# A two-layer encoder kernel: the order of five instruction streams worked out back from the products

## The chip, the cores and the metric

One NeuronCore of a Trainium2 chip runs the whole kernel in one launch. The core has four compute engines, each with its own instruction stream: TensorE (PE in the profile, with its weight loads as PEld) for products and transposes, VectorE (DVE), ScalarE (ACT) and GpSimd (POOL) for work on elements; a fifth stream, SyncE (SP), issues the transfers. Products are written to PSUM, which is used here as eight banks of 128 x 512 floats; everything else lives in SBUF. The metric is the device time of one execution in microseconds, as the median of the runs.

## The reference

Two encoder layers over 512 tokens of width 1024, then a last RMS norm. All inputs are float32. Each layer does, cut to what matters:

```python
h = rms_norm(x, norm_mix)
na_q, na_k, na_v, g_q, g_k, g_v = split(h @ w_in)           # 8 heads each, 64 wide; g_k, g_v have 2
na  = softmax(na_q @ na_k.T / 8 + bias, masked to a window of 8 rows x 16 columns) @ na_v
g_q, g_k = rope(rms_norm(g_q)), rope(rms_norm(g_k))         # per head
gqa = softmax(g_q @ g_k.T / 8) @ g_v                        # 4 query heads share one key head
x = x + concat(na, gqa) @ w_out
x = x + softmax(q @ k.T / sqrt(128)) @ v @ w_mem_o          # q from rms_norm(x), k and v from 256 memory tokens
u = conv3(rms_norm(x) @ w_up)                               # width 3 over the positions, 5632 columns
x = x + (silu(u[:2816]) * u[2816:]) @ w_down
```

## The kernel before

**Products.** A float32 product is made of three faster ones: every operand is split into a rounded part `hi` (type fp32r) and the rest `lo`, and PE adds hi x hi, hi x lo and lo x hi into one PSUM bank. A weight tile arrives in `raw` by a transfer that SP issues; ACT casts it to `hi` (L269, in one or two halves), and POOL, sometimes DVE, subtracts to make `lo` (L270). Both have four buffers, `raw` has two. The activations are held transposed, as operands `xg` (L439, L442). Before a cast can write `hi`, the products that read this buffer's last tile have to be done; before a product can start a new group, its PSUM bank has to be free. There are four banks for products and transposes of attention (`mm`), two for scores (`sc`), two for transposes and small sums (`tr`).

**Stages.** In each layer the neighbourhood heads and the grouped-query heads come first (about 40 to 343 us of the span in the first layer, 686 to 1017 in the second, with the memory attention at their end), then the FFN (343 to 686 and 1017 to 1330). The projections of one head group are woven with the attention of another: a `Filler` hands out products of a projection in portions while softmax work of the former heads goes on.

**The steps that the following parts name.** In the neighbourhood attention L762 adds the bias and reduces, L768 takes the exponential on ACT, L774 and L780 normalise, and the values' products are evicted by a copy on ACT (L814) and two operations on DVE (L815, L816), of which the last one frees the `mm` bank. A grouped-query projection is evicted by L866 and L867 on DVE and L868 on ACT, normalised by L878, L884, L885, L889, rotated and added up by L899, and split by L703 and L705. Grouped-query scores are reduced by L924 (DVE), put through the exponential by L926 (ACT), inverted by L932 (DVE), scaled by L491 (POOL) and, transposed by PE, copied to operands by L484 (ACT) and L485 (DVE). L849 evicts the values, L537 scales a memory operand.

**What sets the order.** PE's products and SP's transfers stand in the order in which the program emits them: their engines are wrapped, and every instruction is pinned.

```python
    def __getattr__(self, name):                      # class InOrder
        op = getattr(self.engine, name)
        return lambda *a, **k: self.tc.keep_in_program_order(op(*a, **k))
```

DVE, POOL and most of ACT are ordered by the framework's scheduler, which plays the program through with its own costs and takes the ready instruction of the best priority. Two devices lean on it: `behind(n)` sets a weight cast back by n places in priority, and `issue_after(closed[-1])` keeps the casts of three kinds of weights (memory queries, FFN up, keys) behind the last closed group.

## Time and profile before

| | |
|---|---|
| time, median of 3 runs (lowest, highest) | 1372.61 us (1371.69, 1373.6) |
| span of the profiled execution, the time it stands for | 1373.2 us |
| instructions | 19238 |
| busy: PE, PEld, DVE, ACT, POOL | 1350.8, 1154.6, 873.9, 676.8, 689.6 us |
| granted TensorE clock, mean | 0.997 |
| transfers | 139.88 MB, mean 102 GB/s |

The page gives no time of the profiled execution but its span, which lies 0.6 us above the median of the runs and among them. A busy share says how long an engine had anything to do; where PE is the engine that is always busy, its idle time between products, with what it waits for, is what is left over.

### The profile page before, as it was taken

What the parts mean: (1) busy time and instruction counts of PE and PEld (TensorE: products, weight loads), DVE (VectorE), ACT (ScalarE), POOL (GpSimd) and SP (SyncE); (2) the same over time, 40 slices, a digit from 0 to 9 for tenths busy, and PEclk for the clock granted to TensorE, in tenths of its full rate; (3) what the DMA queues carried; (4) which work ended last, traced back from release to release, by engine and by line L of the source; (5) the groups of instructions that cost most, each with busy time, mean ns of one, the idle gap of its engine ahead of it and who ended that gap; (6) DMA issues with size and microseconds to landing.
All of it is one profiled execution on the core that took longest, in us unless ns stands there. A gap on an engine that the chain in (4) does not pass through costs nothing.

```text
span 1373.2 us, 19238 instructions
## 1 busy us (share of the span) xinstructions
PE 1350.8 (98%) x7068; PEld 1154.6 (84%) x7068; DVE 873.9 (64%) x1540; ACT 676.8 (49%) x1258; POOL 689.6 (50%) x493
## 2 busy tenths in 40 slices
PE   9999999999999999999999999999999999999997
PEld 7998799888888888888888978998788888888897
DVE  6676675565886188268546767745758833861874
ACT  6775676564543243233457657755554422432441
POOL 2566656626444443444544666657264444444441
PEclk9999999999999999999999999999999999999999
DMA  6763213222333332332265531133143333333331
GB/s 214 230 167 95 62 47 93 84 70 78 107 93 95 104 93 85 107 99 84 86 183 179 150 88 54 57 99 92 32 123 92 93 108 92 93 92 108 92 93 62
DMA packets 219358, 139.88 MB, mean 102 GB/s; under 512 B 6144, under 2 KB 212224, under 8 KB 219264
## 3 DMA queue, kind: packets, MB, share of 16 engines
q1 hardware_dynamic: 218160, 137.99, 34.2%
q8 instruction: 56, 0.92, 0.3%
q10 hardware_dynamic: 1104, 0.66, 0.2%
q14 instruction: 38, 0.31, 0.1%
HBM read 126.05 MB, written 2.10 MB: 93 GB/s over the span
## 4 chain that ended last, share of the span: by engine, by line
PE 90%; DVE 4%; ACT 2%; POOL 1%; DMA 1%; issue 1%; ACTq 0%; DVEq 0%; POOLq 0%
PE mm L76 80%; PE sc L76 6%; PE tr L63 3%; PE tr L76 1%; POOL lo L270 1%; DVE mm L428 1%; DVE xT L429 1%; DMA raw<-in_w_in 0%; ACT hi L269 0%; ACT t L768 0%; DVE r L705 0%; DVE s L924 0%; DVE xg L485 0%; DMA raw<-in_w_mem_q 0%; DVE t L815 0%
## 5 line engine op out<-in xcount | busy, mean ns | idle before, releaser
L270 POOL TENSOR_TENSOR lo<-raw,hi 128x1024 fp32r<-128x1024 f32 (+2 forms) x268 | 500.2, 1877 | 478.0 <-ACT hi L269 477.8
L76 PE MATMUL mm<-xg,hi 128*128 128x512 f32 x1920 | 595.6, 391 | 3.6 <-DVE t L816 2.1
L76 PEld LDWEIGHTS mm<-xg,hi 128*128 128x128 f32 x1920 | 356.3, 188 | 74.7 <-issue 2.3
L269 ACT CAST hi<-raw 128x512 fp32r<-128x512 f32 (+2 forms) x276 | 224.0, 835 | 329.4 <-PE mm L76 271.5
L76 PE MATMUL mm<-xg,lo 128*128 128x512 f32 x960 | 374.0, 390 | 0.0
L76 PE MATMUL mm<-r,hi 128*128 128x512 f32 (+1 forms) x1144 | 331.6, 374 | 2.0 <-DVE xg L442 1.6
L76 PEld LDWEIGHTS mm<-r,hi 128*128 128x128 f32 x1144 | 207.1, 189 | 40.3 <-DVE xg L442 3.3
L1238 DVE SCALAR_TENSOR_TENSOR t<-t,par,t 128x7 f32<-128x7 f32 (+1 forms) x352 | 201.9, 641 | 34.0 <-ACT t L1231 34.0
L76 PE MATMUL mm<-r,lo 128*128 128x512 f32 (+1 forms) x572 | 212.9, 372 | 0.0
L76 PEld LDWEIGHTS mm<-xg,lo 128*128 128x128 f32 x960 | 180.5, 188 | 38.2
L76 PEld LDWEIGHTS mm<-r,lo 128*128 128x128 f32 x572 | 107.8, 188 | 18.8
L1223 DVE TENSOR_TENSOR t<-mm,rep 128x512 f32<-128x512 f32 x88 | 60.1, 687 | 77.7 <-PE mm L76 62.1
L491 POOL TENSOR_SCALAR t<-t,s 128x512 f32<-128x512 f32 (+1 forms) x112 | 66.7, 610 | 72.9 <-DVE s L932 39.6
L1244 DVE TENSOR_TENSOR r<-t,r 128x512 fp32r<-128x512 f32 x44 | 90.4, 2056 | 7.4 <-ACT r L1243 4.3
L1240 ACT ACTIVATE t<-t 128x512 f32<-128x512 f32 x44 | 27.9, 633 | 134.7 <-DVE t L1238 134.6
L1267 DVE TENSOR_TENSOR xT<-xT,mm 128x512 f32<-128x512 f32 x32 | 21.9, 685 | 106.8 <-PE mm L76 106.8
L76 PE MATMUL sc<-r,r 128*128 128x256 f32 (+1 forms) x352 | 71.0, 334 | 1.7 <-ACT t L926 1.7
L1231 ACT ACTIVATE t<-t,par 128x512 f32<-128x512 f32 x88 | 66.8, 806 | 3.3 <-DVE t L1223 3.3
L63 PE MATMUL tr<-ident,t 128*128 128x128 f32 x456 | 63.1, 276 | 3.3 <-DVE s L932 1.2
L63 PEld LDWEIGHTS tr<-ident,t 128*128 128x128 f32 x456 | 53.1, 142 | 12.7 <-issue 5.8
L76 PE MATMUL mm<-r,r 128*128 128x256 f32 (+1 forms) x428 | 62.0, 297 | 0.6 <-DVE r L705 0.6
L76 PEld LDWEIGHTS mm<-r,r 128*128 128x128 f32 x428 | 56.2, 191 | 3.2 <-DVE r L705 0.8
(153 smaller groups left out, 1571.7 us busy)
## 6 DMA issues: line engine op xcount, KB each, us to landing
raw<-in_w_up SPq DMA_DIRECT2D x88, 512.0 KB, 3.7
raw<-in_w_in SPq DMA_DIRECT2D x33, 512.0 KB, 4.2
raw<-in_w_down SPq DMA_DIRECT2D x32, 448.0 KB, 3.6
raw<-in_w_mem_kv SPq DMA_DIRECT2D x16, 512.0 KB, 3.8
raw<-in_w_down SPq DMA_DIRECT2D x16, 512.0 KB, 3.9
r<-in_bias SPq DMA_DIRECT2D x16, 384.0 KB, 5.6
r<-r SPq DMA_DIRECT2D x22, 256.0 KB, 5.1
raw<-in_w_out SPq DMA_DIRECT2D x8, 512.0 KB, 3.6
```

Of the source, the lines that this page charges most:

```text
L63: return lambda *a, **k: self.tc.keep_in_program_order(op(*a, **k))
L76: return self.tc.keep_in_program_order(self.engine.matmul(out, lhsT, rhs, **k))
L269: act.copy(hi[:, k], raw[:, k])
L270: (POOL if eng[0] == "P" else DVE).tensor_sub(lo[:, k], raw[:, k], f(hi)[:, k])
L428: DVE.tensor_add(pm, pm, xT[c])
L491: eng.tensor_scalar(e, e, sums[:, col : col + 1], 1.0, op0=ALU.mult, op1=ALU.mult)
L1223: DVE.tensor_mul(u, us[side], ffn.rep)
L1231: ACT.activation(cc, u, AF.Identity, bias=par[:, l, CB + ch : CB + ch + 1], scale=w[1])
L1238: DVE.scalar_tensor_tensor(cc[:, dst], u[:, src], wi, cc[:, dst], op0=ALU.mult, op1=ALU.add)
L1240: ACT.activation(cs[0], cs[0], AF.Silu)
L1244: DVE.tensor_sub(acts[j][1], cs[0], f(acts[j][0]))
L1267: DVE.tensor_add(xT[m], xT[m], pm)
```

## The change

After the whole program has been emitted, and ahead of the framework's own pass, `put_in_order` makes an order for all five streams. It reads every instruction with the tiles that it reads and writes, and gives each a busy time and a latency from a table of costs by engine, kind and width. From start times of the products (at first PE without any idle time) `due` works back through everything that feeds a product, and through the buffers and banks that have to be free, to the latest time at which each instruction may start. `run` then plays the program forward: an engine takes, among the instructions that could start within its `patience`, the one that is due first; PE takes the first in the program's order among those that could start within 60 ns, and looks 300 instructions ahead. This is done for six plans (with SP's order given or free, and with margins of 0, 40 or 80 ns) and twice for each, from the former round's starts. Each order is then played three times with every operation up to 4% longer and up to 80 ns late at random, and the one of the lowest mean is kept. It is forced on the framework as a chain of dependencies without synchronisation, one per engine. The pins of `InOrder` and the gate `issue_after` go; `behind` stays. The two names `InOrder` and `Counted` remain as plain wrappers. No instruction is added or taken away, but a cast that stood as two halves one after the other can now have other work between.

```diff
 class InOrder:
     def __getattr__(self, name):
         op = getattr(self.engine, name)
-        return lambda *a, **k: self.tc.keep_in_program_order(op(*a, **k))
+        return op
...
+PLANS = [
+    ((60.0, 300.0, 300.0, 300.0, 0.0), 300, given, margin) for given in ((), (E_SP,)) for margin in (0.0, 40.0, 80.0)
+]
...
+    def due(self, start):
+        later = [[] for _ in self.steps]
+        for tag, tiles in self.opened.items():
+            for a, b in zip(tiles, tiles[self.bufs[tag]:]):
+                first = self.users[b][0]
+                for x in self.users[a]:
+                    if x < first:
+                        later[x].append(first)
...
+        for s in reversed(self.steps):
+            long = HANDOVER + (s.busy + LANDING + s.moved / BYTES_PER_NS if s.moved else s.length)
+            for x in s.frees:
+                same = self.steps[x].engine == s.engine and not s.moved
+                at[s.i] = min(at[s.i], at[x] - (s.busy if same else long))
+            for x in later[s.i]:
+                at[s.i] = min(at[s.i], at[x] - long)
+        return at
...
+                if e in held:
+                    i = program[e][head[e]]
+                    among = (i,) if not todo[i] else ()
+                else:
+                    reach = program[e][min(head[e] + ahead, len(program[e]) - 1)] if e == E_PE else len(steps)
+                    among = [i for i in open_to[e] if i <= reach]
...
+                if can:
+                    soon = min(can)[0] + patience[e]
+                    _, t, i = min((due[i] if due and e != E_PE else i, t, i) for t, i in can if t <= soon)
...
+def put_in_order(tc):
...
+    for patience, ahead, given, margin in PLANS:
+        at = start
+        for _ in range(2):
+            r = course.run(course.due(at), patience, ahead, given, margin)
...
+            under = [course.run(None, (0.0,) * 5, 0, order=r[2], rng=np.random.default_rng(n)) for n in range(3)]
...
+            mean = sum(u[0] for u in under) / len(under)
+            if best is None or mean < best[0]:
+                best = mean, r[2]
+    order = best[1]
+    follows = mybir.DependencyInfo(mybir.DependencyClass.NoSync, mybir.DependencyReason.DATA)
+    for engine in order:
+        for a, b in zip(engine, engine[1:]):
+            tc.add_manual_dep(course.steps[b].ins, course.steps[a].ins.name, follows, reason="put_in_order")
...
-                with tc.issue_after(closed[-1]) if closed and key[0] in ("memq", "up", "k") else nullcontext():
-                    act.copy(hi[:, k], raw[:, k])
+                act.copy(hi[:, k], raw[:, k])
...
     with tile.TileContext(nc, schedule_with_timeline_sim=True) as tc:
         encoder_kernel(tc, t, out)
+        put_in_order(tc)
```

What it makes of the order at three places; a row reads line, operation, output <- inputs with the numbers of the tiles, and shape. The lines of the changed kernel have other numbers, since the planner stands ahead of them.

**Third query projection of the second layer, about 804 us of the span, DVE.** `mm_7572` and `mm_7580` are the two banks with the products of the attention values, `t_7570` their result; `mm_7603` holds the rotated queries, `t_7601` the grouped-query values. Before:

```order
L878 SCALAR_TENSOR_TENSOR s_7564<-tr_7559,geps 128x8
L899 TENSOR_TENSOR mm_7603<-t_7441,mm_7603 128x512
L815 TENSOR_TENSOR t_7571<-mm_7572,t_7571 64x2x128
L815 TENSOR_TENSOR t_7571<-mm_7580,t_7571 64x2x128
L816 TENSOR_TENSOR t_7570<-mm_7572,t_7571 64x256
L849 TENSOR_TENSOR t_7601<-mm_7522,rep_6368 128x512
L816 TENSOR_TENSOR t_7570<-mm_7580,t_7571 64x256
```

Now (L1096 and L1097 are L815 and L816, L1130 is L849, L1180 is L899, L766 is L485):

```order
L1096 TENSOR_TENSOR t_7571<-mm_7572,t_7571 64x2x128
L1097 TENSOR_TENSOR t_7570<-mm_7572,t_7571 64x256
L1130 TENSOR_TENSOR t_7601<-mm_7522,rep_6368 128x512
L1180 TENSOR_TENSOR mm_7603<-t_7441,mm_7603 128x512
L766 TENSOR_TENSOR r_7634<-tr_7629,r_7634 128x512
L1096 TENSOR_TENSOR t_7571<-mm_7580,t_7571 64x2x128
L1097 TENSOR_TENSOR t_7570<-mm_7580,t_7571 64x256
```

The eviction of the first bank moved ahead of L899, and that of the second bank behind it. On ACT the copies L814 of both banks moved ahead of the cast of `hi_7694`.

**The same place, PE.** `mm_7616` is the projection that takes over a bank of the values, `tr_7629` and `tr_7637` are transposes. Before:

```order
L76 MATMUL mm_7616<-xg_5998,hi_7420 128x512
L76 MATMUL mm_7616<-xg_5999,hi_7420 128x512
L76 MATMUL mm_7616<-xg_5998,lo_7421 128x512
L63 MATMUL tr_7629<-ident,t_7409 128x128 x4
L63 MATMUL tr_7637<-ident,t_7410 128x128 x4
```

Now:

```order
L77 MATMUL mm_7603<-ident,t_7454 128x128 x4
L1071 MATMUL tr_7629<-ident,t_7409 128x128 x4
L1071 MATMUL tr_7637<-ident,t_7410 128x128 x3
L77 MATMUL mm_7616<-xg_5998,hi_7420 128x512
L77 MATMUL mm_7616<-xg_5999,hi_7420 128x512
L77 MATMUL mm_7616<-xg_5998,lo_7421 128x512
```

Six products of the projection stood ahead of the eight transposes; now seven of the eight stand ahead of the projection.

**First layer, about 120 us, ACT.** `sc_1381` and `sc_1382` are scores of the neighbourhood attention, `mm_1320` is the projection that L868 evicts, `hi_1525` and `hi_1437` are weight casts. Before:

```order
L269 CAST hi_1525<-raw_1318 128x512 x2
L768 ACTIVATE t_1393,s_1392<-sc_1381,s_1391 128x256 x2
L768 ACTIVATE t_1394,s_1392<-sc_1382,s_1391 128x256 x2
L868 ACTIVATE t_1410<-mm_1320 128x512
L814 COPY t_1415<-mm_1416 64x2x128
L814 COPY t_1415<-mm_1424 64x2x128
```

Now (L1049 is L768, L550 is L269, L1149 is L868, L1095 is L814):

```order
L550 CAST hi_1437<-raw_1214 128x512 x2
L1049 ACTIVATE t_1393,s_1392<-sc_1381,s_1391 128x256
L1049 ACTIVATE t_1394,s_1392<-sc_1382,s_1391 128x256
L1049 ACTIVATE t_1393,s_1392<-sc_1381,s_1391 128x256
L1049 ACTIVATE t_1394,s_1392<-sc_1382,s_1391 128x256
L550 CAST hi_1525<-raw_1318 128x512
L1149 ACTIVATE t_1410<-mm_1320 128x512
L1095 COPY t_1415<-mm_1416 64x2x128
L1095 COPY t_1415<-mm_1424 64x2x128
```

The four exponentials moved ahead of the cast of `hi_1525`, and its second half behind the evictions. On PE the scores moved 42 rows ahead.

**First layer, about 154 us, ACT.** `sc_1767` and `sc_1768` are grouped-query scores, `sc_1806` and `sc_1807` the next ones, which take over their banks. `hi_1998` takes over the buffer of `hi_1525`, which the products of `mm_1781` read. Before:

```order
L926 ACTIVATE t_1776,s_1774<-sc_1767,s_1773 128x512
L926 ACTIVATE t_1779,s_1774<-sc_1768,s_1773 128x512
L926 ACTIVATE t_1815,s_1813<-sc_1806,s_1812 128x512
L926 ACTIVATE t_1818,s_1813<-sc_1807,s_1812 128x512
L269 CAST hi_1998<-raw_1732 128x512 x2
```

Now (L1207 is L926, L984 is L703):

```order
L550 CAST hi_1998<-raw_1732 128x512
L1207 ACTIVATE t_1776,s_1774<-sc_1767,s_1773 128x512
L1207 ACTIVATE t_1779,s_1774<-sc_1768,s_1773 128x512
L550 CAST hi_1998<-raw_1732 128x512
L984 CAST r_1887<-mm_1827 64x512
L1207 ACTIVATE t_1815,s_1813<-sc_1806,s_1812 128x512
L1207 ACTIVATE t_1818,s_1813<-sc_1807,s_1812 128x512
```

One half of the cast moved ahead of the exponentials of the first pair, the other ahead of the second pair. On PE the order at this place is, before:

```order
L63 MATMUL tr_1789<-ident,t_1717 128x128 x4
L63 MATMUL tr_1796<-ident,t_1720 128x128 x4
L76 MATMUL sc_1806<-r_1506,r_1635 128x512 x2
L76 MATMUL sc_1807<-r_1507,r_1635 128x512 x2
L76 MATMUL mm_1781<-r_1502,hi_1525 128x512 x2
L76 MATMUL mm_1781<-r_1502,lo_1526 128x512
L76 MATMUL mm_1781<-r_1722,hi_1525 128x512 x2
L76 MATMUL mm_1781<-r_1722,lo_1526 128x512
```

Now (`mm_1841` is the projection group that follows `mm_1781`, `mm_1827` another transpose):

```order
L1228 MATMUL tr_1789<-ident,t_1717 128x128 x4
L77 MATMUL mm_1781<-r_1722,hi_1525 128x512
L1228 MATMUL tr_1796<-ident,t_1720 128x128 x4
L77 MATMUL mm_1781<-r_1722,hi_1525 128x512
L77 MATMUL mm_1781<-r_1722,lo_1526 128x512
L77 MATMUL mm_1827<-ident,t_1681 128x128 x4
L77 MATMUL mm_1841<-r_934,hi_1611 128x512 x2
L77 MATMUL mm_1841<-r_934,lo_1612 128x512
L77 MATMUL sc_1806<-r_1506,r_1635 128x512 x2
```

The rest of `mm_1781` and the first products of `mm_1841` moved ahead of the scores `sc_1806`.

## The prediction

> **What bounds the kernel now.** I read the busy times and the chain that ended last first, then the windows by stage, then TensorE's (PE's) waits, and then the timeline at the longest of them.

> ```profile
> PE 1350.8 (98%) x7068; PEld 1154.6 (84%) x7068; DVE 873.9 (64%) x1540; ACT 676.8 (49%) x1258; POOL 689.6 (50%) x493
> PE 90%; DVE 4%; ACT 2%; POOL 1%; DMA 1%; issue 1%; ACTq 0%; DVEq 0%; POOLq 0%
> ```

> PE is busy for 98% of the span and holds 90% of the chain; no other engine is above 64%. So an order can bring only what PE loses between products, and that is found stage by stage. In the windows the columns are the stretch, its length, the busy time of PE, PE's weight loads, VectorE (DVE), ScalarE (ACT) and GpSimd (POOL), then the granted clock, the DMA share and GB/s.

> ```profile
> 0.00:40.00 40.00, 37.23 (x181) 31.50 (x182) 27.23 (x48) 26.45 (x47) 12.30 (x15) 1.00 0.63 196
> 40.00:343.00 303.00, 296.12 (x1757) 258.29 (x1757) 195.26 (x417) 189.15 (x426) 181.51 (x166) 1.00 0.35 103
> 343.00:686.00 343.00, 343.00 (x1515) 284.12 (x1515) 217.50 (x301) 131.91 (x172) 155.15 (x71) 1.00 0.33 96
> 686.00:1017.00 331.00, 326.32 (x1918) 285.54 (x1918) 207.91 (x435) 202.06 (x445) 191.41 (x174) 0.99 0.36 105
> 1017.00:1330.00 313.00, 313.00 (x1416) 260.62 (x1415) 202.94 (x280) 117.96 (x150) 138.40 (x59) 1.00 0.33 97
> 1330.00:1373.20 43.20, 35.11 (x290) 34.55 (x288) 23.02 (x61) 9.30 (x21) 10.79 (x9) 0.94 0.21 69
> ```

> The two FFN stretches have no idle PE at all (343.00 of 343.00, 313.00 of 313.00): nothing is to be had there. The two attention stretches lose 303.00 − 296.12 = 6.88 and 331.00 − 326.32 = 4.68, together 11.56 us. The first 40 us wait for the first loads and the last 43 for the closing norm; they idle for 2.77 and 8.09, in single chains with no other work to put in the gaps, and I take nothing from them. What PE waits for between 40 and 1017 (total, times, longest):

> ```profile
> PE mm L76 <- DVE t L816: 2.1, 1, 2.1
> PE sc L76 <- ACT t L926: 1.7, 2, 1.4
> PE mm L76 <- DVE xg L442: 1.6, 4, 0.4
> PE mm L76 <- ACT t L868: 1.5, 1, 1.5
> PE tr L63 <- DVE s L932: 1.2, 3, 0.7
> PE tr L63 <- DVE t L491: 1.1, 3, 0.4
> PE mm L76 <- DVE r L705: 0.6, 1, 0.6
> PE tr L63 <- DVE xg L485: 0.5, 1, 0.5
> PE tr L76 <- DVE r L485: 0.4, 1, 0.4
> PE tr L63 <- DVE s L563: 0.4, 1, 0.4
> PE mm L76 <- POOL r L505: 0.3, 1, 0.3
> ```

> That is 11.4 us in 19 waits, none for a DMA: small evictions and softmax steps that come late behind other work on DVE and ACT.

> **The ceiling.** Idle time understates a wait. The place of the longest one (third query projection of the second layer) shows by how much; columns are start, duration, engine, line, operation, tiles, and in brackets the idle time before.

> ```profile
> 798.72 0.76 PE L76 MATMUL mm<-r,r 128*128 128x256 f32 x5
> 799.09 1.85 DVE L537 SCALAR_TENSOR_TENSOR r<-r,par,r 128x256 fp32r<-128x256 f32 x2
> 800.02 0.63 PE L76 MATMUL mm<-xg,hi 128*128 128x512 f32 x2
> 800.48 0.39 PE L76 MATMUL mm<-xg,lo 128*128 128x512 f32 x1
> 800.68 1.14 ACT L269 CAST hi<-raw 128x512 fp32r<-128x512 f32 x2 [2.13 <-PE mm L76]
> 801.73 0.75 ACT L814 COPY t<-mm 64x256 f32<-64x256 f32 x2
> 801.86 0.70 DVE L899 TENSOR_TENSOR mm<-t,mm 128x512 f32<-128x512 f32 x1 [0.72 <-issue]
> 802.46 0.86 DVE L815 TENSOR_TENSOR t<-mm,t 64x256 f32<-64x256 f32 x2
> 803.35 0.42 DVE L816 TENSOR_TENSOR t<-mm,t 64x256 f32<-64x256 f32 x1
> 803.91 0.70 PE L76 MATMUL mm<-xg,hi 128*128 128x512 f32 x2 [2.15 <-DVE t L816]
> 805.00:808.30 3.30, 3.30 (x13) 2.81 (x12) 0.69 (x1) 1.20 (x3) 0.89 (x1) 0.50 0.38 106
> ```

> A product lasts 0.39 us, but in a row of them the next starts after (800.48 − 800.02)/2 = 0.23, so a wait loses its idle time plus the overlap, 0.39 − 0.23 = 0.16: for 19 waits 3.0 us. And the window row shows the granted clock at 0.50 for 3.30 us right after this wait, when half the work is done: 1.65 us more. Ceiling: 11.56 + 3.04 + 1.65 = 16.25 us.

> [...]

> **The change, part by part.** It adds and takes away no product, cast or transfer; each engine gets a new fixed order, and the gate that held some weight casts back until an earlier group was closed goes. SP's transfers keep their order exactly. PE keeps most of its order; DVE, ACT and POOL are reshuffled. Waiting instructions change with it: 873 to 900 on PE, 1289 to 1150 on DVE, 881 to 841 on ACT. A wait that is met in time costs PE nothing (the FFN stretches hold hundreds and no idle time), so I price the 27 more at 0; if every one came just late they would cost 27 × 0.16 = 4.3. A change of the loads' times I also price at 0: no row of PE's waits above names a DMA, and the order of the queue stays.

> *Longest wait, 803.91.* The products of the attention values end about 799.5. Then ACT stands 2.13 us in front of a weight cast (L269) which needs a buffer from PE; behind it wait the two copies L814, behind these DVE's L899, L815, L816, and only the first L816 frees the bank of the next products. In the new order L814 stands ahead of that cast, L815 and L816 of the first bank stand ahead of L849 and L899, and seven ready transposes fill PE in front of the products. DVE's L537 still ends at 799.09 + 1.85 = 800.94; L815 (0.86/2 = 0.43) and L816 (0.42) follow, so the bank is free near 801.9. PE ends its row at 801.76 and has seven transposes, at 1.04/8 = 0.13 each (row below), to do: 802.6. Margin 0.7. Gain 2.15 + 0.16 + 1.65 = 3.96.

> ```profile
> 151.96 1.04 PE L63 MATMUL tr<-ident,t 128*128 128x128 f32 x8
> 154.40 1.40 PE L76 MATMUL sc<-r,r 128*128 128x512 f32 x4 [1.40 <-ACT t L926]
> 116.53 1.14 ACT L269 CAST hi<-raw 128x512 fp32r<-128x512 f32 x2 [2.80 <-PE mm L76]
> 117.50 0.74 DVE L867 SCALAR_TENSOR_TENSOR t<-mm,qkg,r 128x512 f32<-128x512 f32 x1
> 117.52 1.06 PE L76 MATMUL mm<-ident,t 128*128 128x128 f32 x8
> 118.94 0.48 ACT L768 ACTIVATE t<-sc,s 128x256 f32<-128x256 f32 x1
> 119.39 0.60 ACT L868 ACTIVATE t<-mm 128x512 f32<-128x512 f32 x1
> 120.04 0.73 PE L76 MATMUL mm<-xg,hi 128*128 128x512 f32 x2 [1.47 <-ACT t L868]
> ```

> *154.40.* PE has transposed the last scores' probabilities and waits for a score bank that two exponentials (L926) free. The new order puts six products (6 × 0.23 = 1.4) and another group of eight transposes (about 1.04) between the first of these transposes and the next scores. But on ACT half a cast now stands ahead of the two exponentials, and it waits for the third of the six: from there PE has 1.04 + 3 × 0.23 = 1.7 us to do, ACT 1.14/2 = 0.57 and an exponential of 0.7. After 0.2 or so for the handovers the margin is about 0.2. The row L926 has 1.7 us in two waits; with the one of 0.5 (L485) that follows from it, 2.2 + 3 × 0.16 = 2.68.

> *120.04.* PE waits for L868, which ACT does after a cast of 1.14 and four exponentials; the scores of these move 42 rows ahead on PE, so the exponentials come ahead of the cast, and of the cast, which still starts at 116.53, only one half (0.57) stays in front of L868. L868 then ends near 117.7 instead of 119.99, the other user of the bank, L867, at 117.50 + 0.74 = 118.24, and PE is there at 120.04 − 1.47 = 118.57: margin 0.3. Gain 1.47 + 0.16 = 1.63.

> *Two more.* The longest wait for L932 (0.7, at 839) goes as its cast and subtraction move forward: 0.86. The one for L705 (0.6, at 141) has four small products (sums over pairs of columns) put in front: 0.76.

> These five places give 3.96 + 2.68 + 1.63 + 0.86 + 0.76 = 9.89. The other waits are worth 16.25 − 9.89 = 6.36, all of 0.2 to 0.5 us. Followed by hand nearly all go, but by margins of 0.05 to 0.3 us, so I take half: 3.2. For the same reason I put in two new waits that miss by 0.1: 2 × (0.1 + 0.16) = 0.5. Sum: 9.9 + 3.2 − 0.5 = 12.6. The profiled execution (span 1373.2) lies 0.6 above the median and inside the runs' spread, so the same sum is taken off the median: 1372.6 − 12.6 = **1360.0**.

> **The rivals.**

> *Casts at the head of ACT's queue (slower).* What went wrong at 803.91 can be made elsewhere: a cast put early stands still until PE gives its buffer back, and an exponential or eviction that PE needs stands behind it. ACT's waits of this kind, first in the window 40 to 343, then in 686 to 1017:

> ```profile
> ACT hi L269 <- PE mm L76: 13.2, 8, 2.9
> ACT hi L269 <- PE mm L76: 16.4, 12, 2.9
> ```

> That is 20 waits and 29.6 us, 1.48 each, up to 2.9. Before, nearly all of them stood where ACT had nothing urgent. The new order, without the gate, cuts casts into halves and puts several directly ahead of exponentials (154.40 is one). If eleven of the 20 held a product by their mean, 16.3 − 12.6 = +3.7: 1376.3. It decides from nine (13.3 > 12.6). For it: the margins are tenths, and the planner's lateness of up to 80 ns for an operation is less than the 0.7 idle "issue" of L899 above. Against it: the planner moves along with PE's products, and at the five places worked out no cast is late.

> [...]

> *Only the longest waits go.* The three above 1 us give 3.96 + 1.63 + 1.56 = 7.15, and the small ones come back elsewhere as banks and buffers pass to other tiles: 1365.5. For it: 16 of the 19 waits are under 0.8 us and depend on tenths.

> *Nothing gained.* Waits move, the sum stays: 1371 to 1374. The order does reach the instruction streams, so the change does what it says; that it would cancel to within 2.7 us needs an accident.

> *All of it.* The ceiling with no new wait: 1372.6 − 16.25 = 1356.4.

> **How the numbers follow.** A change of 0.2%, 2.7 us, is about what a measurement of this kernel can tell from none. Forecast (1357 to 1363) 0.52; all of it (1355 to 1357, with the runs' spread of a microsecond) 0.08; only the longest (1363 to 1370) 0.20; nothing gained 0.06; casts at the head 0.14. Faster: 0.52 + 0.08 + 0.20 = 0.80. The same three make the range, 1355 to 1370; the two left out are 0.20. The 27 waits' upper price of 4.3 and the clock's term lie inside it.

> **What would show it.** Right: PE's idle time falls to some 3 us in 40 to 343 and 1 to 2 in 686 to 1017, L816 and L868 are gone from its waits, no clock of 0.50 stands in the window near 805, and the FFN stretches stay at full. The forecast is wrong if PE's waits name L926, L932 or the evictions more often than before, with ACT idle in front of a cast until just before; if PE idles in an FFN stretch, because an order has put a weight cast too late; or if waits for a DMA appear.

## The result and the profile after

The changed kernel takes 1366.95 us, the median of 4 runs (1366.41 to 1367.23), beside 1373.11 for the kernel before on the same chips: the ratio is 0.995, its 95% interval 0.9934 to 0.9965. That is 6.2 us faster where 12.6 were forecast. The profiled execution has a span of 1365.2 us, 8.0 less than before. In every run that lists both, the time is 1.7 to 1.9 us longer than the span. So the profiled execution of the kernel before, with a span of 1373.2, stands for about 1375.0 us, some 2 above the median and not 0.6, and the spans differ by more than the medians. The page of the changed kernel, busy times and chain:

```profile
PE 1345.2 (99%) x7068; PEld 1154.7 (85%) x7068; DVE 909.3 (67%) x1540; ACT 680.0 (50%) x1258; POOL 695.4 (51%) x493
PE 94%; DVE 2%; DMA 1%; ACT 1%; issue 1%; POOL 1%; SPq 0%; ACTq 0%; DVEq 0%; POOLq 0%
```

PE's share of the chain rose from 90 to 94%. DVE's busy time rose by 35 us with the same instructions, which no part of the prediction had. Some 29 us of that lie in the FFN stretches, where PE never idles (342.00 of 342.00 us and 312.00 of 312.00 are busy), and their lengths did not change. By stretch (after: the first attention in two pieces, then the second; then the same two pieces of the first before):

```profile
40.00:150.00 110.00, 103.06 (x633) 91.02 (x633) 73.11 (x176) 69.33 (x173) 65.50 (x69) 0.99 0.58 161
150.00:341.00 191.00, 190.08 (x1108) 166.54 (x1107) 127.28 (x242) 120.54 (x253) 117.71 (x101) 1.00 0.24 71
683.00:1010.00 327.00, 327.00 (x1939) 288.71 (x1938) 211.04 (x438) 204.64 (x449) 193.06 (x174) 1.00 0.36 107
```

```profile
40.00:150.00 110.00, 107.10 (x662) 95.07 (x663) 74.82 (x183) 71.82 (x179) 69.76 (x72) 1.00 0.55 158
150.00:343.00 193.00, 189.02 (x1097) 163.22 (x1095) 120.45 (x234) 117.33 (x247) 111.76 (x95) 1.00 0.24 72
```

The second layer's attention lost every wait: 327.00 of 327.00 busy, where it had idled for 4.68. From 150 us on the first layer idles for 0.92 instead of 3.98. But between 40 and 150 us PE now idles for 6.94 instead of 2.90. PE's waits between 40 and 341 us are all there is:

```profile
PE mm L77 <- DVE r L766: 2.6, 2, 1.6
PE mm L77 <- ACT t L1149: 1.7, 1, 1.7
PE mm L77 <- DVE r L986: 1.6, 2, 1.0
PE tr L1418 <- DVE t L772: 0.9, 1, 0.9
PE tr L1071 <- DVE s L844: 0.9, 1, 0.9
PE tr L77 <- DVE r L766: 0.8, 1, 0.8
```

To set the kernels side by side, I take from each trace the place where PE has started 181, 843, 1938, 3453, 5371 and 6787 instructions and begins the next one (about 40, 150, 343, 687, 1018 and 1331 us before). Up to each place the kernels have done the same mix of products (pipe and port differs by 0.1 to 0.2 us of them in two stretches). Each column is the change of a stretch against before, in us; the last runs to the end of the span. The columns are read from one profiled execution each, the medians from all runs.

| kernel | median, us | to 40 | 40-150 | 150-343 | FFN | 687-1018 | FFN | end |
|---|---|---|---|---|---|---|---|---|
| after | 1366.95 | -0.1 | **+6.1** | -5.3 | 0.0 | -8.9 | -0.1 | +0.3 |
| products held | 1372.22 | +6.0 | -1.7 | -1.8 | 0.0 | -7.4 | +0.2 | +1.4 |
| transfers free | 1358.75 | +0.3 | -2.7 | -5.3 | 0.0 | -9.2 | -0.1 | +0.6 |
| one pipe | 1358.68 | +0.5 | -3.3 | -5.3 | 0.0 | -9.2 | -0.1 | +1.0 |
| pipe and port | 1362.05 | +0.5 | -2.6 | -6.7 | 0.0 | -3.3 | +0.2 | +2.0 |
| casts behind | 1361.16 | -1.4 | -1.1 | -5.3 | 0.0 | -8.8 | -0.1 | +1.0 |
| bias early | 1360.02 | +0.2 | -1.6 | -5.3 | 0.0 | -8.9 | -0.1 | +0.5 |
| gate alone | 1375.0 | -1.1 | +1.0 | +0.3 | 0.0 | -0.9 | 0.0 | +0.2 |
| products planned | 1382.33 | +2.8 | +6.5 | -0.9 | 0.0 | -1.7 | -0.3 | +1.3 |
| cast later | 1357.79 | +0.3 | -3.3 | -6.4 | 0.0 | -9.2 | -0.1 | +1.3 |
| par first | 1357.27 | +0.4 | -2.5 | -6.4 | 0.0 | -9.2 | -0.1 | +0.8 |
| pipe, wide port | 1357.27 | +1.0 | -3.3 | -6.4 | 0.0 | -9.2 | -0.1 | +0.3 |

The first 40 us vary by some 1.5 us from run to run (after and "casts behind" have the same order there; in the one the granted clock was 0.50 for 3.4 us of the first 40, and its mean over the execution is 0.995, where the other has 0.997), so small differences are read from the other columns.

**Where the 6.1 us come from.** The largest new waits of PE are at 62.57 and 64.01 us, for splits by DVE. The timeline there, ACT, DVE and PE:

```profile
56.16 0.63 ACT L833 ACTIVATE t<-t 128x512 f32<-128x512 f32 x1 [3.42 <-DMA t<-in_memT]
58.85 1.14 ACT L550 CAST hi<-raw 128x512 fp32r<-128x512 f32 x2 [1.66 <-DMA raw<-in_w_in]
59.90 1.17 ACT L984 CAST r<-mm 64x512 fp32r<-64x512 f32 x2
61.10 1.07 ACT L765 CAST r<-tr 128x512 fp32r<-128x512 f32 x2
59.51 1.29 DVE L551 TENSOR_TENSOR lo<-raw,hi 128x512 fp32r<-128x512 f32 x2 [6.44 <-ACT hi L550]
61.82 0.69 DVE L766 TENSOR_TENSOR r<-tr,r 128x512 fp32r<-128x512 f32 x1
62.57 0.50 PE L77 MATMUL mm<-r,r 128*128 128x256 f32 x2 [1.64 <-DVE r L766]
64.01 0.50 PE L77 MATMUL mm<-r,r 128*128 128x256 f32 x2 [0.95 <-DVE r L766]
```

ACT stands 3.42 us for a load of the memory tokens and 1.66 more for a weight, and DVE 6.44 behind ACT; the evictions that the products need (L984, L765) stand behind both. The products of that weight, `hi_701`, begin at 77 us. A window shows the two engines empty and the DMA engines full:

```profile
54.00:56.00 2.00, 2.00 (x13) 1.72 (x12) 0.00 (x0) 0.00 (x0) 0.56 (x2) 1.00 1.11 257
```

The weight was issued at 49.29. A DMA row of 0.1 to 0.2 us around that issue gives its size and the time to landing; then the same for the load issued at 49.54 before:

```profile
raw<-in_w_in SPq DMA_DIRECT2D x1, 512.0 KB, 9.5
```

```profile
raw<-in_w_in SPq DMA_DIRECT2D x1, 512.0 KB, 4.5
```

SP's transfers have the same order in both. What differs is the pause in front of that weight. SP's rows before, then after:

```profile
30.51 9.87 SPq L63 DMA_DIRECT2D raw<-in_w_in  x3
43.33 0.71 SPq L63 DMA_DIRECT2D t<-in_memT  x1
49.54 0.38 SPq L63 DMA_DIRECT2D raw<-in_w_in  x1
```

```profile
29.72 13.59 SPq L533 DMA_DIRECT2D raw<-in_w_in  x3
46.85 0.76 SPq L831 DMA_DIRECT2D t<-in_memT  x1
49.29 0.39 SPq L533 DMA_DIRECT2D raw<-in_w_in  x1
```

Each time three weights come first, then six transfers of memory tokens, bias and shifts inside SBUF, then the weight in question. The last of the three is issued by 40.4 us before and by 43.3 after. SP waits there for POOL's subtractions, which give the buffers of `raw` back and follow ACT's casts; they end at 40.0 before and at 42.9 after. So the six follow 2.9 to 3.5 us later. The weight behind them waits for a subtraction too, which ends at nearly the same time in both; what SP waits for between the six and the weight, before and after:

```profile
SPq L63 <- POOL lo L270: 5.4, 1, 5.4
```

```profile
SPq L533 <- POOL lo L551: 1.6, 1, 1.6
```

From the issue of the last of the six to that of the weight, the time in which they drain shrank from 6.2 to 2.4 us.

Idle time is 4.0 of the 6.1 us (6.94 less 2.90). Another 1.7 us is the clock, by my estimate from 3.4 us at 0.50, in which a product of 512 columns starts 0.43 us after the one before (148.34 to 148.77) and not 0.23; they began 1.4 us behind the last of PE's waits:

```profile
146.33 0.73 PE L77 MATMUL mm<-r,r 128*128 128x256 f32 x4 [0.98 <-DVE r L986]
147.70:151.10 3.40, 3.40 (x10) 2.62 (x9) 2.46 (x6) 1.57 (x3) 2.15 (x2) 0.50 0.07 19
```

Whether the other three runs had this too is not on record; they list a mean clock of 0.996 to 0.997 instead of 0.995, and took the same time within 0.6 us.

### The profile page after: what moved, and what is told of

Same layout as the page of the kernel before. It is cut to its first block, busy times and chain, and to the rows that moved or that the text cites. A ratio compares the mean times of both kernels' runs of the same rounds, so it can differ in the third digit from the quotient of the medians.

```text
span 1365.2 us, 19258 instructions
## 1 busy us (share of the span) xinstructions
PE 1345.2 (99%) x7068; PEld 1154.7 (85%) x7068; DVE 909.3 (67%) x1540; ACT 680.0 (50%) x1258; POOL 695.4 (51%) x493
## 4 chain that ended last, share of the span: by engine, by line
PE 94%; DVE 2%; DMA 1%; ACT 1%; issue 1%; POOL 1%; SPq 0%; ACTq 0%; DVEq 0%; POOLq 0%
PE mm L77 83%; PE sc L77 6%; PE tr L1228 2%; PE tr L77 1%; PE tr L1071 1%; DMA raw<-in_w_in 1%; PE tr L1418 1%; POOL lo L551 0%; DMA t<-t 0%; DVE r L818 0%; DMA par<-in_par 0%; ACT r L984 0%; ACT hi L550 0%; ACT r L966 0%; DVE r L766 0%
## 5 line engine op out<-in xcount | busy, mean ns | idle before, releaser
L550 ACT CAST hi<-raw 128x512 fp32r<-128x512 f32 (+2 forms) x276 | 225.8, 837 | 302.3 <-PE mm L77 232.2
L1519 DVE SCALAR_TENSOR_TENSOR t<-t,par,t 128x504 f32<-128x504 f32 (+1 forms) x352 | 287.7, 859 | 18.7 <-ACT t L1512 15.8
L1524 ACT CAST r<-t 128x512 fp32r<-128x512 f32 x44 | 27.3, 620 | 78.4 <-DVE t L1522 78.4
L1525 DVE TENSOR_TENSOR r<-t,r 128x512 fp32r<-128x512 f32 x44 | 48.1, 1092 | 17.2 <-ACT r L1524 16.5
L77 PEld LDWEIGHTS sc<-r,r 128*128 128x128 f32 x352 | 52.1, 190 | 5.3 <-ACT t L1049 0.4
L1205 DVE TENSOR_REDUCE s<-sc 128x1 f32<-128x512 f32 x64 | 43.5, 686 | 19.0 <-PE sc L77 18.9
```

What stands on the lines that cost most here:

```text
L77: return self.engine.matmul(out, lhsT, rhs, **k)
L550: act.copy(hi[:, k], raw[:, k])
L1205: DVE.tensor_reduce(nmx[:, c], sc[j], axis=AX.X, op=ALU.max, negate=True)
L1519: DVE.scalar_tensor_tensor(cc[:, dst], u[:, src], wi, cc[:, dst], op0=ALU.mult, op1=ALU.add)
L1524: ACT.copy(acts[j][0], cs[0])
L1525: DVE.tensor_sub(acts[j][1], cs[0], f(acts[j][0]))
```

## The experiments

Each run is compared with the kernel before on the same chip.

**Products held.** The planner with PE in the program's order; its choice among the plans has SP free.

```diff
-    ((60.0, 300.0, 300.0, 300.0, 0.0), 300, given, margin) for given in ((), (E_SP,)) ...
+    ((60.0, 300.0, 300.0, 300.0, 0.0), 300, given, margin) for given in ((E_PE, E_SP), (E_PE,)) ...
```

> The planner, but with the products held in the order in which the program emits them; only ACT, DVE, POOL (and the transfers) are planned. Theory (the second attention layer lost its waits because products that are ready were put in front of products that wait, and the other engines were put in order for that): most of the gain goes, 1370 to 1376 us, with several us of idle PE back in the second layer's attention, L816 and L926 among its waits. Rival (the order of evictions and casts on ACT and DVE did it, the products hardly matter): 1365 to 1368 and no more than 1 us idle there.

It measured 1372.22, ratio 0.9994 (0.9985 to 1.0002). The time was as the theory had it, but not for its reason: the second layer got 7.4 of its 8.9 us without moving a product, as the rival said. Most of the gain was given back in the first 40 us (+6.0), where PE waited 2.5 us for a cast and 1.6 for a subtraction that are needed early in the program's order, and where the granted clock was 0.96 in the mean. Beside the run with free transfers, which differs in the products' order, 150 to 343 us gains 1.8 instead of 5.3: there the products do matter.

**Products planned.** The complement: only PE and SP in the planned order, the rest as before.

```diff
-    for engine in order:
+    for engine in (order[E_PE], order[E_SP]):
...
+                with tc.issue_after(closed[-1]) if closed and key[0] in ("memq", "up", "k") else nullcontext():
```

> Products and transfers in the changed kernel's order, ACT, DVE and POOL left to the framework as before, with the gate. Theory (after the run with held products: the order of ACT and DVE took most of the waits from the second attention layer, the products' order mattered for the first 25 us and for single places): the second layer keeps over 3 us of idle PE, and the time is 1367 to 1376 us. Rival (products in front of waits are enough): under 1 us idle there and 1362 to 1367.

1382.33, ratio 1.0058 (1.0045 to 1.007): slower than either limit, though the second layer keeps 4.7 us of PE's waits, as the theory said. The loss lies in the first 150 us: PE waits 2.8 us there for one eviction by ACT, and the clock is at 0.75 from 120 to 121 us and at 0.50 from there to 126. The second layer gains 1.7 us only, and the wait for the last value eviction is back (L1098 is L816 here):

```profile
PE mm L77 <- DVE t L1098: 2.4, 1, 2.4
```

So the order of ACT and DVE took away the second layer's waits; that of the products alone does not pay.

**Gate alone.** The kernel before without `issue_after`.

```diff
-                with tc.issue_after(closed[-1]) if closed and key[0] in ("memq", "up", "k") else nullcontext():
-                    act.copy(hi[:, k], raw[:, k])
+                act.copy(hi[:, k], raw[:, k])
```

> The kernel before without the gate that holds three kinds of weight casts back; products and transfers pinned, the rest ordered by the framework. Theory (the gate's going is no part of the gain; it only lets casts stand at the head of ACT's queue): 1371 to 1378 us. Rival (the gate was what held casts, and with them evictions, too late): 1364 to 1369.

1375.0, ratio 1.0006 (0.9997 to 1.0015): no part of the gain.

**Casts behind.** The changed order, transfers and all, with five rows moved.

```diff
+MOVES = [(E_ACT, ("t_74_537", "hi_105_701"), "r_94_642"), (E_DVE, ("lo_106_702",), "r_94_642")]
```

> The changed kernel's own order with five rows moved: on ACT the scaling of a memory tile and the two halves of the cast of hi_701 (whose products start at 77 us) go from in front of the splits of mm_547, tr_629 and tr_637 to behind them; on DVE the two subtractions of that cast likewise. The transfers stay as they are and land as late. Theory (the loads' lateness costs time only because casts that nobody needs yet stand in front of work that products wait for): the waits at 62.57 and 64.01 (2.9 us) go, and part of the 1.0 at 90.8 and the 0.9 at 111: 1362 to 1364.5 us. Rival (the crowd on the transfers itself is what products wait for): 1366 to 1368, as after.

1361.16, ratio 0.9904 (0.989 to 0.9917), 5.8 us under the changed kernel (on another chip) and more than expected: in 40 to 150 us the loss of 6.1 became a gain of 1.1, read from the fastest of its four executions (1359.21). The weight lands as late (9.0 us) and ACT waits 1.71 for it, but with the evictions done:

```profile
52.14 1.16 ACT L992 CAST r<-mm 64x512 fp32r<-64x512 f32 x2
53.32 1.07 ACT L773 CAST r<-tr 128x512 fp32r<-128x512 f32 x2
56.97 1.14 ACT L558 CAST hi<-raw 128x512 fp32r<-128x512 f32 x2 [1.71 <-DMA raw<-in_w_in]
```

L992 is L984 and starts 7.8 us sooner, 1.4 of it from the earlier start. The waits at 90.8, 111 and 146 us, which I had counted apart, were mostly the tail of this one: the only wait of PE above 0.5 us that is left between 40 and 150 is the one for L1149 (1.7).

**Bias early.** The changed order with two loads moved into SP's pause at 30 us.

```diff
+MOVES = [(E_SP, ("r_64_454", "r_65_455"), "raw_41_314")]
```

> The changed kernel's own order with two rows moved, on SP: the two loads of bias that it issues at 44.0 and 45.1 go in front of the weight load at 40.4, into the pause of SP from 30 to 40 us. Theory (a crowd of transfers between 43 and 62 us makes the weight load of 49.3 take 9.5 us instead of 4.5): it lands 2 to 3.5 us sooner, the waits at 62.57 and 64.01 shrink from 2.9 to under 1.2 us: 1362.5 to 1365.5 us. Rival (the loads are late because SP issues them late, behind a buffer): no change, 1366 to 1368.

1360.02, ratio 0.99 (0.9885 to 0.9915). The weight, issued at 49.55, lands in 4.3 us, five sooner than in the changed kernel and more than the theory had, and both waits are gone. So the lateness is the crowd's, and either cure is enough: a thinner crowd, or nothing urgent behind it.

**Transfers free.** The same costs, only the plan that may order SP too.

```diff
-... for given in ((), (E_SP,)) for margin in (0.0, 40.0, 80.0)
+... for given in ((),) for margin in (80.0,)
```

> The planner unchanged in its costs, but only the plan in which it may order SP's transfers too (margin 80). Theory (the waits between 40 and 150 us come from loads that land 4 to 5 us later than the planner takes them to, so that ACT stands in front of them): the planner knows no better here, so 3 to 8 us of idle PE stay in 40 to 150: 1363 to 1369 us. Rival (the held order of the transfers is what made the loads late): idle PE in 40 to 150 under 2 us, 1359 to 1361.

1358.75, ratio 0.9892 (0.9879 to 0.9906): the rival held, a little under its range, and the theory's conclusion that the planner "knows no better" was wrong. It needs no better model where it may spread the transfers itself.

**One pipe.** Transfers inside SBUF share the pipe of the others in the planner, whose rate for memory goes from 280 to 260 bytes per ns.

```diff
-                if s.inside:
-                    end += s.moved / 90.0
-                else:
-                    memory = max(memory, t + busy) + s.moved / BYTES_PER_NS
-                    end = max(end, memory + LANDING + 12.0 * late[i])
+                if s.inside:
+                    end += s.moved / 110.0
+                memory = max(memory, t + busy) + s.moved / (150.0 if s.inside else BYTES_PER_NS)
+                end = max(end, memory + LANDING + 12.0 * late[i])
```

> The planner with another model of the transfers: those from SBUF to SBUF go through the same pipe as those from memory (at 150 B/ns, beside 260 for memory), so that a crowd delays all. Theory: PE's idle time in 40 to 150 falls from 6.9 us to under 3, ACT no longer waits more than 2 us for loads of w_in there, and the time is 1360 to 1364 us; the wait near 283 us (DVE held by POOL) stays. Rival (the waits come from small misses in the engines' costs, which this does not touch): 1365 to 1368, as after.

1358.68, ratio 0.9894 (0.988 to 0.9907). The planner now chose a plan with free transfers, so its time equals that of the run above, which kept the old model, and does not show that the new one itself brings anything.

**Pipe and port.** Beside it, the planner lets DVE instructions that read SBUF through two operands, or scale a wide one, stand until POOL stops (`port` is that time in its code), through POOL's next instructions too if these are ready by then; POOL's narrow instructions are left out of this.

```diff
-            wide = [a for a in reads if columns(a) > 16]
+            wide = [a for a in reads if columns(a) > 1]
...
-                    busy += max(0.0, port - t)
+                    hold = max(port, t)
...
+                        for x in queue[:4]:
...
+                            if todo[x] or ready[x] > hold or steps[x].opens and not (room(steps[x]) or 0.0) <= hold:
+                                break
+                            hold += steps[x].busy
+                    busy += hold - t
```

> As the kernel of the one pipe, and the planner also knows that a DVE instruction with two operands in SBUF, narrow ones too, or a wide scaling of one, stands until POOL has no instruction running, through several in a row. Theory: DVE's busy time falls back from 909 us towards 874 and the waits near 146 and 283 us go, another 1 to 2 us off the kernel of the one pipe: 1358 to 1362. Rival (these two waits were chance, and the stricter rule costs order elsewhere): the same or up to 3 us slower than the one pipe.

1362.05, ratio 0.9915 (0.9901 to 0.9929): the rival held, with 3.4 us more than the one pipe where it said up to 3. 150 to 343 us gained another 1.4, but DVE's busy time stayed (911.4 us) and a wait of 2.81 came up at 796 us. There half a cast stands ahead of the copies, as at 803.9 before (L1106 is L814). On DVE, L1191 and L777 stand for 1.2 us between L1107 and L1108 (L815 and L816), twice what the half cast takes:

```profile
793.25 0.63 ACT L561 CAST hi<-raw 128x512 fp32r<-128x512 f32 x1
793.90 0.76 ACT L1106 COPY t<-mm 64x256 f32<-64x256 f32 x2
794.30 0.42 DVE L1107 TENSOR_TENSOR t<-mm,t 64x256 f32<-64x256 f32 x1 [2.19 <-ACT t L1106]
794.64 0.68 DVE L1191 TENSOR_TENSOR mm<-t,mm 128x512 f32<-128x512 f32 x1
795.24 0.68 DVE L777 TENSOR_TENSOR r<-tr,r 128x512 fp32r<-128x512 f32 x1
795.84 0.41 DVE L1108 TENSOR_TENSOR t<-mm,t 64x256 f32<-64x256 f32 x1
796.39 0.76 PE L77 MATMUL mm<-xg,hi 128*128 128x512 f32 x1 [2.81 <-DVE t L1108]
797.40:800.80 3.40, 3.40 (x10) 2.63 (x9) 2.38 (x5) 0.00 (x0) 0.18 (x1) 0.50 0.50 154
```

The profiled execution is the slowest of the five (1365.12). The clock was at 0.50 from the end of that wait (796.4) to 800.8 and at 0.64 from there to 803, which by my estimate from these two figures costs about 3 us; the two fastest runs, at 1361.6 and 1361.7, list a mean clock of 0.998 and not 0.995. So the -3.3 of this row in the table probably holds some 3 us that the median does not have.

**Cast later, par first, wide port.** Three small ones. On the free transfers, the cast of `hi_601` goes behind two exponentials, and then ACT's parameter load in front of its first weight load as well. The third is the one pipe with the wider rule for DVE, but for one POOL instruction at a time.

```diff
+MOVES = [(E_ACT, ("hi_601_3262",), "s_591_3213")]
...
+MOVES = [(E_ACT, ("hi_601_3262",), "s_591_3213"), (E_ACT, ("raw_1_89",), "par_84")]
```

> The kernel with free transfers, with one row moved: on ACT the cast of hi_601 (products from 290 us) goes behind the exponentials of t_592, so that POOL starts its subtraction of 2.4 us some 3.5 us later. Theory (DVE's scaling of t_588 took 1.53 us instead of 0.35 because POOL's subtraction was running, and PE waited 1.07 for it at 275 us): the scaling takes under 0.5 us, the wait shrinks below 0.4: 1357.7 to 1358.5 us. Rival (the next scaling meets the subtraction instead): the wait moves on by 2 to 5 us and the time stays at 1358.5 to 1359.2.

> The same, and on ACT's own queue the small parameter load goes in front of the first weight load, as in the kernel before. PE's first product waits for ACT's scaling of the first activation tile, which waits for the parameters 1.17 us (5.65 us of the span, 1.69 us lost). Theory: the scaling starts 0.4 to 0.5 us sooner and so does everything: another 0.3 to 0.6 us off, 1357.2 to 1358.2. Rival (the weight load is then as late as the parameters were): no change.

> The planner of the one pipe, and the rule that DVE instructions with two narrow operands or one wide scaled operand in SBUF also stand while POOL runs, POOL's narrow instructions excepted, but for one POOL instruction at a time (no rows of them, as in the kernel of pipe and port). Theory (the stricter rule for rows of POOL instructions made that kernel's order worse at 796 us, not the port itself): no wait over 0.5 us near 275, 146 and 796, 1356.5 to 1358.3 us. Rival: 1358.5 to 1360, as the one pipe.

1357.79 (ratio 0.9883, 0.9867 to 0.99), 1357.27 (0.9879, 0.9864 to 0.9894) and 1357.27 (0.9882, 0.9867 to 0.9897). The two scalings at 273 us, with free transfers and then with the cast later:

```profile
273.61 1.79 DVE L772 TENSOR_SCALAR t<-t,s 128x256 f32<-128x256 f32 x2
```

```profile
272.98 0.62 DVE L780 TENSOR_SCALAR t<-t,s 128x256 f32<-128x256 f32 x2
```

The wait went as expected, and 1.1 us of that stretch with it. The third kernel gains the same 1.1 us by its rule, and no wait over 0.6 us is left near 275, 146 or 796. Whether the early parameter load brings anything is open: PE's first product started 0.41 us sooner, but the place behind its 181st instruction did not come sooner. The last two are the fastest here, 1.2% under the kernel before.

## Why the prediction was right in sign and half wrong in size

- **Bounds.** Right. The FFN stretches did not move, the end by 0.3.
- **Ceiling.** Too low. The two stretches apart from 40 to 150 us gained 14.1 us; of the ceiling of 16.25, 3.5 lay in 40 to 150 (2.9 idle and four overlaps), so they gained 1.4 more than the 12.7 that I saw in them. The span of the wide port is 1355.5, 17.7 less than before. So a wait cost more than its idle time and 0.16 us; what the rest is stays open.
- **The sum.** By the spans, 40 to 150 us lost 6.1 where the terms of the sum gain about 3, and the rest gained about 4 more than its terms: 8.0 in place of 12.6. The medians have 6.2, because the profiled execution before took about 2 us more than its median. I had put that at 0.6, reading its span as its time.
- **803.91.** Right for the wait: 6.00 of 6.00 us busy there. It is the order of ACT and DVE that does it, since with the products alone the wait stays.

```profile
800.00:806.00 6.00, 6.00 (x37) 5.15 (x36) 5.81 (x11) 4.06 (x10) 5.94 (x6) 1.00 0.25 84
```

- **The clock's term (1.65).** Not a price of that wait: with the gate alone the same 2.15 us of idle PE came at 804.11, and the clock stayed at 1.00.

```profile
805.00:808.40 3.40, 3.40 (x21) 2.90 (x20) 1.32 (x4) 2.13 (x4) 0.94 (x1) 1.00 0.37 113
```

  Between the two profiles the term was gained at 805 and lost again at 147.7; that it stood in the sum at all was the chance of one execution.
- **154.40, 163.55 and 839.4.** Right: no wait for L1207 (L926) or for the reciprocal is left, and behind 150 us none for L766 (L485).
- **120.04.** Wrong: the wait is there, at 124.25, with 1.7 us. I let the exponentials and the cast move on ACT and took the end of DVE's L867 from the old timeline. But on DVE four score reductions and two scalings (L818) had moved ahead of it:

```profile
119.23 0.17 DVE L1159 SCALAR_TENSOR_TENSOR s<-tr,geps 128x8 f32<-128x8 f32 x1 [1.15 <-PE tr L77]
121.48 0.76 DVE L818 SCALAR_TENSOR_TENSOR r<-r,par,r 128x256 fp32r<-128x256 f32 x1
122.82 0.74 DVE L1148 SCALAR_TENSOR_TENSOR t<-mm,qkg,r 128x512 f32<-128x512 f32 x1
```

  L1159 stands for PE, the reductions and L818 behind it, and L1148 (L867) starts at 122.82, where I had it at 117.50. With the casts behind and with the bias early the wait stays at 1.7, so it is the plan's own loss.
- **140.9.** Wrong: PE waits 1.0 us there, at 146.33, because DVE's L818 took 3.80 us, where its other fifteen took 0.47 to 1.12 (below). The wait is gone in both kernels that undo the late loads or what they hold up, so it was a chance meeting that these brought about.
- **The small waits, taken half (3.2).** Too low: from 150 us on all of them went, and one new one of 0.9 came, for a scaling by DVE.
- **"A change of the loads' times I also price at 0: no row of PE's waits above names a DMA, and the order of the queue stays."** This is the step that failed, with the 0.5 us put in for new waits. The order of a queue says nothing of its times: the same order, without the pause that a late buffer had forced on it, made a load of 4.5 us one of 9.5. The stretch cost 6.1 where it gains 2.7 with free transfers; with five rows of ACT and DVE moved it gains 1.1, and with two loads issued earlier 1.6. The sign that I had named, PE waiting for a DMA, never came: the loads stopped ACT, and PE's rows name the casts and splits behind it.
- **The rival of casts at the head of ACT's queue.** Its mechanism came, but for loads instead of PE's buffers. ACT's waits between 40 and 150 us:

```profile
ACT hi L550 <- DMA raw<-in_w_in: 3.6, 3, 1.7
ACT t L833 <- DMA t<-in_memT: 3.4, 1, 3.4
```

  PE's buffers held up casts for only 0.5 us there. I had bounded the rival by the row that names PE and left out the rows that name DMA. Going by size, the result lies nearest to "only the longest waits go" (1365.5), but none of its mechanism is there: the small waits went, and one of the long ones stayed.

## What to carry to other kernels

An order that is planned from instruction costs has to be priced with its transfers: look at what the issue queue waits for before, and at what it will issue together once that wait is gone. A cast of a load that nobody needs for 15 us should not stand in front of an eviction on the same engine (here ACT stood 3.42 and 1.66 us for loads, with two evictions behind); place it behind, or let the planner move the transfer as well. When the order of one engine is followed by hand, every other engine on the path has to be read in its new order too, not at its old time. And a half clock in one profiled execution is not yet a price of the wait in front of it: look for the same wait in another run first.

## What the runs showed of the hardware

**DVE stood behind POOL, through several instructions.** L818, which reads two operands from SBUF, took 3.80 us:

```profile
133.51 3.80 DVE L818 SCALAR_TENSOR_TENSOR r<-r,par,r 128x256 fp32r<-128x256 f32 x1
133.27 1.29 POOL L551 TENSOR_TENSOR lo<-raw,hi 128x512 fp32r<-128x512 f32 x1
134.52 1.28 POOL L1170 TENSOR_TENSOR t<-t,t 128x512 f32<-128x512 f32 x1
135.76 1.27 POOL L551 TENSOR_TENSOR lo<-raw,hi 128x512 fp32r<-128x512 f32 x1
```

**Half clock after short idle times.** The granted clock fell to 0.50 after PE had idled for 2.15 us at 803.91 before, and after 0.98 us at 146.33 in the changed kernel; in pipe and port it stood at 0.50 when PE went on after the wait of 2.81. It stayed at 1.00 after the same 2.15 us with the gate alone (the row above), and with the products planned after the 2.4 us in front of 814:

```profile
815.20:818.50 3.30, 3.30 (x16) 2.67 (x15) 1.55 (x3) 1.64 (x3) 0.00 (x0) 1.00 0.25 88
```

So in these five places, with waits of 1.0 to 2.8 us, the length of the wait alone does not decide it. The half clock lasted 3.4 us in the first two, and in the third at least the 4.4 us from 796.4 to 800.8.

**In a crowd a load took 9.5 us instead of 4.5.** Issued 2.4 us behind the last of six transfers, a weight of 512 KB took 9.5 us, with a DMA share of 1.07 over that time. Issued 6.2 us behind them it took 4.5 (share 0.84), and with two of the six moved away 4.3, though the share was 1.03 from 49 to 50 us. So here what had been issued shortly before told more than the share did.
